# Stick-breaking attention: sums over later keys as two float32r products on the logits' bank, and a new order of the tail

## The chip, the cores and the metric

One core of one Trainium2 chip runs the whole program. The metric is the device time of one execution in microseconds (us).

## The reference, cut to what matters

Two small transformer blocks run one after the other on a sequence of 256 tokens of width 1024, all in float32. The last-but-one stage is stick-breaking attention with 16 heads of 64:

```python
def stick_breaking(h, w_in, q_gain, k_gain, w_o):
    q, k, v = jnp.split(h @ w_in, 3, axis=-1)
    q = rms_norm(heads(q), q_gain); k = rms_norm(heads(k), k_gain); v = heads(v)
    for blk in range(S // QB):                      # two blocks of 128 queries
        z = einsum('bhtd,bhsd->bhts', q[blk], k[:kend]) * scale
        mask = s_pos[None, :] < t_pos[:, None]
        log_stay = where(mask, log_sigmoid(-z), 0.0)
        later = cumsum(log_stay, axis=3, reverse=True) - log_stay
        weight = where(mask, exp(log_sigmoid(z) + later), 0.0)
        outs.append(einsum('bhts,bhsd->bhtd', weight, v[:kend]))
    return concatenate(outs) @ w_o
```

With softplus(z) = max(z, 0) + log(1 + exp(-|z|)), log_sigmoid(-z) is -softplus(z) and log_sigmoid(z) is z - softplus(z). So the weight of a key is exp(z - softplus(z) - sum of softplus over the later keys).

## The kernel before, in words

The tokens lie in two halves of 128 partitions. All weights stream from HBM in slabs of 128x2048 float32. Each slab is split into a float32r high part (cast on ACT, L168) and a low part (subtraction on VectorE, L169), and every product of the projections is made of three float32r matmuls (high-high, high-low, low-high: L271 to L273 for projections by columns, L294 to L300 for output products). A call of W.pump splits the next slab and sends off the load of another on SP's queue.

The framework (Tile) orders the instructions of TensorE, VectorE and POOL by itself, from the order in the program and its estimate of what is ready. It also hands out the buffers of a pool: those of one tag are given to the next tile in the order in which they come free. For stages 8 and 9 the ACT engine is taken out of that (L1388): ACT executes in the order in which the program is written.

Stage 8, `stick`, is the attention. Its projection `si` has six chunks of 512 columns, done in the order q (2), k 2, v 4, k 3, v 5. `both(c, ...)` (L1243) does one chunk in four steps (two slab halves times two token halves, twelve matmuls each), and after each step the attention work that is listed for it. Heads are taken in pairs, i = 0 to 7; e is the head in the pair. The logits z of one head are 128 keys by 3x128 columns: the second key block for the second query block, then the first key block for both query blocks. The work on a pair:

- `l1(i)` (L1158): mask and logits into the bank (L1168 to L1172, TensorE), then on ACT l = Abs(z), Exp(-l), Ln(1 + l) (L1186 to L1188). The banks are a two-bank tile, acc0 for even pairs and acc1 for odd ones; pair 6 takes the two `mm` banks of the projections.
- `l2(i)` (L1191), VectorE: sp = max(z, 0) + l, which is softplus (L1194), and l = min(z, 0) - l, which is log_sigmoid(z) (L1195).
- `w1(i)` (L1197): sums over later keys, float32 products of the constant `later` with sp, written over z in its bank (L1201 with 384 columns, L1202 with 128), then l = l - sum on VectorE (L1204).
- `w2(i)` (L1206), ACT: the weight, Exp(l) in place. The text calls it weight Exp(i).
- `pv(i)` (L1210): weights times v (L1222), then the split of the result into high and low parts for the output product (ACT L326, VectorE L327).

The tiles l and sp of pairs 0 to 5 come from the pool `k4` (one tag, four buffers of 4 KB per partition), which the other stages use too for their 4 KB tiles. Those of pairs 6 and 7 lie in one tile of the pool `xt`.

In the tail (L1280) `out(j, half)` is the j-th quarter of the output product for one token half, in acc0 or acc1, with pair work behind it. The next stage's first steps (residual, norm, transposes) follow.

Of the kernel before, what the change touches and what calls it, by code (L numbers as in the profile page):

```python
# [11 lines left out]
F32 = mybir.dt.float32  # L12
F32R = mybir.dt.float32r
# [5 lines left out]
P = 128  # L19
# [172 lines left out]
def tile_two_models(ctx: ExitStack, tc: tile.TileContext, a: dict):  # L192
# [3 lines left out]
    def pool(name, bufs, **kw):  # L196
        return ctx.enter_context(tc.tile_pool(name=name, bufs=bufs, **kw))
# [3 lines left out]
    part_pool = pool("part", SLOTS)  # L201
    xt_pool = pool("xt", 1)
    k8 = pool("k8", 1)
    k4 = pool("k4", 4)
    k2 = pool("k2", 4)
    wk = pool("wk", 2)
    sm = pool("sm", 4)
# [35 lines left out]
    def power(dst, src, add):  # L243

        n = src.shape[-1]
        t = small(n, tag=f"pw{n}")
        V.tensor_scalar(t, src, add, None, ALU.add)
        G.tensor_tensor(dst, t, nhalf[:, 0:n], ALU.pow)

    def junk(n):  # L250
        return wk.tile([P, D], mybir.dt.bfloat16, tag="junk", name="junk", bufs=1)[:, 0:n]
# [125 lines left out]
    def add_normed(gb, weight):  # L377
        def update(half, acc, factor=None):
            eps = EPS / weight**2 if factor is None else factor[1]
            ms = small(2, tag="ms2")  # L380
            y = k4.tile([P, D], F32, tag="k4", name="y")
# [46 lines left out]
    def ffn(tag, xT, rstd, skew=True, first=None, last_stage=False):  # L428
# [41 lines left out]
        def gated(c, b):  # L470

            if c not in hT:
                hT[c] = k4.tile([P, 2, 2, 2, P], F32R, tag="k4", name=f"hT{c}")
# [12 lines left out]
            V.tensor_tensor(hd, t[1], sg, ALU.mult)  # L486
            split_plain(hd, hT[c][:, :, 0, b], hT[c][:, :, 1, b])

        def tr(c, half):
            if c not in hT:  # L490
                hT[c] = k4.tile([P, 2, 2, 2, P], F32R, tag="k4", name=f"hT{c}")
# [114 lines left out]
    def conv(xT, rstd):  # L606
# [9 lines left out]
        def tr_u(c, half):  # L616
            if half not in uT:
                u = big((4, 0)[half], [P, 2048], F32, f"uT{half}")
                uT[half] = u[:, 0 : KD * (P + 2)].rearrange("p (k t) -> p k t", k=KD)
                cv[half] = k4.tile([P, KD, P], F32, tag="k4", name=f"cv{half}")  # L620
                if half == 0:
                    V.memset(uT[0][:, :, 0:2], 0.0)
            t = new_tr("tr_u")
# [99 lines left out]
    def attention(xT, rstd, xk, rstd_k, kT):  # L723
# [38 lines left out]
        def s1(g, half):  # L762
            nh, n = (4, P) if half == 0 else (2, 2 * P)
            ps = new_acc(g % 2, f"sc{half}{g}").rearrange("p (c h k) -> p h c k", h=nh, c=2)
            for i in range(nh):
                hd = g * nh + i
                for c in range(2):
# [4 lines left out]
            s = k4.tile([P, nh, 2, n], F32, tag="k4", name="s")  # L772
# [18 lines left out]
        def s3(g, half):  # L791
            nh, n, s, sums = st.pop((g, half))
            sv = sums.rearrange("p (h c) -> p h c", c=2)
            if half not in r0s:
                r0s[half] = small(8, tag=f"r0{half}")
                if half == 0:
                    asb[half] = k4.tile([P, 8, n], F32, tag="k4", name="aA")
# [143 lines left out]
    def retention(xT, rstd):  # L941
# [21 lines left out]
        rope = k4.tile([P, 2, 2, P], F32, tag="k4", name="rope")  # L963

        G.dma_start(rope, a["rope"].rearrange("p (a b t) -> p a b t", a=2, b=2))

# [59 lines left out]
            ys[hd, half] = y  # L1026

        def tr_y(hd, half):
            y = k4.tile([P, 2, 4, P], F32R, tag="k4", name=f"ryT{hd}_{half}")
# [71 lines left out]
    def stick(xT, rstd):  # L1101
# [17 lines left out]
        mask = k2.tile([P, 3 * P], F32, tag="k2", name="smask")  # L1119
        gq = small(tag="gq", bufs=1)  # L1120
        identr = wk.tile([P, 4 * P], F32R, tag="gb", name="sbr", bufs=1)
        later = wk.tile([P, 2 * P], F32, tag="sg", name="later")

        G.dma_start(mask, a["sb_mask"])
        G.dma_start(later, a["sb_later"])

        def setup():
            S.copy(identr[:, 0:P], ident)
            S.copy(identr[:, P : 4 * P], mask)
            V.scalar_tensor_tensor(gq, g_cols(G_SBQ, 1), 0.125, g_cols(G_SBK, 1), ALU.mult, ALU.mult)  # L1130

        def after(c, half, ps):
# [25 lines left out]
        def l1(i):  # L1158

            if i == 6:  # L1160
                zs = [new_mm() for _ in range(2)]
            else:
                z = new_acc(i % 2, f"z{i}")
                zs = [z[:, 0:512], z[:, 512:1024]]
# [6 lines left out]
            for e in range(2):  # L1171
                T.matmul(zs[e][:, P : 3 * P], k[pp[e], 0:P], q[pp[e], :], start=False, stop=True)  # L1172
            if i < 6:
                l, sp = (k4.tile([P, D], F32, tag="k4", name=n)[:, 0 : 6 * P] for n in ("l", "sp"))
            else:
                if i == 6:
                    st["last"] = xt_pool.tile([P, 2, 2, 6 * P], F32, tag="xT", name="l67")
                t = st["last"][:, i - 6]
                l, sp = t[:, 0], t[:, 1]
            l, sp = (t.rearrange("p (e t) -> p e t", e=2) for t in (l, sp))  # L1180
            if i == 6:
                zp = [(zs[e][:, 0 : 3 * P], l[:, e], sp[:, e]) for e in range(2)]
            else:
                zp = [(z.rearrange("p (e t) -> p e t", e=2)[:, :, 0 : 3 * P], l, sp)]
            for zz, ll, _ in zp:
# [3 lines left out]
            st[i] = zs, zp, l, sp  # L1189

        def l2(i):  # L1191

            for z, l, sp in st[i][1]:
                V.scalar_tensor_tensor(sp, z, 0.0, l, ALU.max, ALU.add)  # L1194
                V.scalar_tensor_tensor(l, z, 0.0, l, ALU.min, ALU.subtract)  # L1195

        def w1(i):  # L1197

            zs, zp, l, sp = st[i]
            for e in range(2):  # L1200
                T.matmul(zs[e][:, 0 : 3 * P], later[:, 0:P], sp[:, e], start=True, stop=False)  # L1201
                T.matmul(zs[e][:, 2 * P : 3 * P], later[:, P : 2 * P], sp[:, e, 0:P], start=False, stop=True)  # L1202
            for z, ll, _ in zp:
                V.tensor_tensor(ll, ll, z, ALU.subtract)  # L1204

        def w2(i):  # L1206
            l = st[i][2]
            S.activation(l, l, AF.Exp)

        def pv(i):  # L1210
            w = st.pop(i)[2]
            t = new_tr("tr_o")
            pp = [slice(0, 64), slice(64, P)]
            c = [slice((2 * i + e) * 64, (2 * i + e) * 64 + 64) for e in range(2)]
            steps = [
# [24 lines left out]
        def body():  # L1240
            nc.scalar.preload_act_table_set("natural_log_exp_and_others")

            def both(c, *todo):  # L1243
# [17 lines left out]
                [(pv, 2), (w2, 3), (l1, 5), (l2, 4)],  # L1261
                [(pv, 3), (w1, 4), (l2, 5)],
            )
            l1(6)

        def out(j, half, *todo):
            def run():
# [11 lines left out]

        tails = [  # L1280
            [
                out(0, 0, (w2, 4), (w1, 5), (l1, 7), (l2, 6)),
                out(1, 0, (w2, 5), (pv, 4), (w1, 6), (l2, 7)),
                lambda: (pv(5), w2(6), w1(7)),
                out(2, 0, (pv, 6), (w2, 7)),
                out(0, 1, (pv, 7)),
                out(3, 0),
            ],
# [5 lines left out]
    def start(make, gcols):  # L1294
        xT, rstd = {}, {}
        stage = make(xT, rstd)
        x_t = [k4.tile([P, 2, 4, P], F32, tag="k4", name=f"x_t{i}") for i in range(2)]
# [109 lines left out]
def constants():  # L1407
# [14 lines left out]
    seen = s_pos // 64 <= t_pos // 64  # L1422
    decay = np.exp(log_gamma[None, :, None] * np.abs(t_pos - s_pos)[:, None, :]) * seen[:, None, :]
    sb_mask = np.where(s_pos < t_pos, 0.0, -1e30).astype(f32)
    sb_later = np.concatenate([p[:, None] > p[None, :], np.ones((P, P))], axis=1).astype(f32)
    return {
        "neg_dist": neg_dist,
        "rope": rope,
# [22 lines left out]
```

## Time and profile before

| | us |
|---|---|
| median of 3 runs (1598.68 to 1600.39) | 1599.68 |
| the profiled execution | 1599.57 |
| its span, first to last instruction | 1597.6 |
| TensorE busy / VectorE / ACT in the span | 1564.9 / 1091.7 / 928.8 |
| stage 8 after its head, about | 1318 to 1412 |

The profiled execution took 2 us more than its span, for what lies before the first and after the last instruction. In the views, PE is TensorE's matmuls, PEld its weight loads, DVE VectorE, ACT ScalarE, SP the queue that issues the loads. A matmul's time in a row includes its drain, so matmuls overlap: the pace is the distance of the starts. A float32 product appears as two records. "x12" is several instructions of one line that follow each other; [1.70 <-PE z L1172] is idle time of the engine before the row and what ended it.

### The profile page before, as it was taken

Reading aid. Unit: us, or ns where it says so; the run is one execution under the profiler, and the core shown is the slowest. Engines: PE = TensorE matmul, PEld = TensorE weight load, DVE = VectorE, ACT = ScalarE, POOL = GpSimd, SP = SyncE. Lnnn points to the kernel's source line nnn. Section 1 sums busy time; section 2 is a strip of 40 time slices with the busy share of each in tenths; the row PEclk is TensorE's granted clock in tenths of the full one; section 3 lists DMA queues with packets and bytes.
Section 4 is the critical chain, followed back from the end, with each engine's and each line's share of the span. In section 5 each row is a group of like instructions: output and inputs, shape, how many; then the busy total and the mean of one; then the engine's idle time right before and its main releaser. Section 6 shows DMA issues by size and latency. Waiting matters only on the chain.

```text
span 1597.6 us, 21722 instructions
## 1 busy us (share of the span) xinstructions
PE 1564.9 (98%) x8408; PEld 1375.4 (86%) x8408; DVE 1091.7 (68%) x1757; ACT 928.8 (58%) x1623; POOL 61.1 (4%) x65
## 2 busy tenths in 40 slices
PE   6999999999999999989999999999999999999999
PEld 6899888899989999877899888888899988688997
DVE  7767767667687676788676776456667676666664
ACT  7655656555576555676555654456455576755552
POOL 0000100000000000101000010000000021000000
PEclk9999999999999999999999999999999999999999
DMA  8755644555655555444555555545455553235551
GB/s 308 254 193 209 235 151 181 198 211 192 207 179 201 211 200 206 159 167 147 183 198 205 212 203 184 185 147 196 160 209 195 207 213 133 105 132 211 207 192 49
DMA packets 42872, 300.94 MB, mean 188 GB/s; under 512 B 4800, under 2 KB 4928, under 8 KB 7312
## 3 DMA queue, kind: packets, MB, share of 16 engines
q1 hardware_dynamic: 42336, 297.91, 52.2%
q8 instruction: 66, 1.08, 0.3%
q0 software_dynamic: 432, 1.64, 0.3%
q14 instruction: 38, 0.31, 0.1%
HBM read 298.48 MB, written 1.05 MB: 187 GB/s over the span
## 4 chain that ended last, share of the span: by engine, by line
PE 88%; DVE 5%; ACT 4%; issue 1%; POOL 1%; DMA 0%; SPq 0%; ACTq 0%; POOLq 0%
PE mm L462 25%; PE mm L465 13%; PE acc L300 8%; PE acc L294 8%; PE acc L297 8%; PE mm L271 7%; PE mm L273 7%; PE mm L272 7%; DVE wlo L169 2%; PE tr L587 1%; ACT whi L168 1%; POOL r L389 1%; PE tr_x L335 1%; PE z L1201 1%; ACT s L786 1%
## 5 line engine op out<-in xcount | busy, mean ns | idle before, releaser
L169 DVE TENSOR_TENSOR wlo<-raw,whi 128x1024 fp32r<-128x1024 f32 x532 | 635.5, 1221 | 324.4 <-ACT whi L168 323.8
L168 ACT CAST whi<-raw 128x1024 fp32r<-128x1024 f32 x532 | 539.7, 1050 | 333.6 <-issue 134.3
L462 PE MATMUL mm<-xT,whi 128*128 128x512 f32 x1856 | 606.3, 383 | 12.5 <-DVE xT L320 12.5
L465 PE MATMUL mm<-xT,wlo 128*128 128x256 f32 x1856 | 469.6, 273 | 0.0
L462 PEld LDWEIGHTS mm<-xT,whi 128*128 128x128 f32 x1856 | 338.6, 190 | 51.2 <-DVE xT L320 12.4
L465 PEld LDWEIGHTS mm<-xT,wlo 128*128 128x128 f32 x1856 | 355.7, 192 | 12.4
L271 PE MATMUL mm<-whi,xT 128*128 128x512 f32 x456 | 178.9, 392 | 0.6 <-ACT xT L318 0.6
L273 PE MATMUL mm<-whi,xT 128*128 128x512 f32 x456 | 173.4, 380 | 0.0
L272 PE MATMUL mm<-wlo,xT 128*128 128x512 f32 x456 | 173.1, 380 | 0.0
L294 PE MATMUL acc<-whi,hT 128*128 128x512 f32 x516 | 153.8, 380 | 0.0
L300 PE MATMUL acc<-whi,hT 128*128 128x512 f32 x516 | 153.7, 379 | 0.0
L297 PE MATMUL acc<-wlo,hT 128*128 128x512 f32 x516 | 153.5, 379 | 0.0
L297 PEld LDWEIGHTS acc<-wlo,hT 128*128 128x128 f32 x516 | 97.5, 189 | 13.8
L300 PEld LDWEIGHTS acc<-whi,hT 128*128 128x128 f32 x516 | 97.5, 189 | 13.8
L294 PEld LDWEIGHTS acc<-whi,hT 128*128 128x128 f32 x516 | 97.4, 189 | 12.2
L271 PEld LDWEIGHTS mm<-whi,xT 128*128 128x128 f32 x456 | 86.2, 189 | 14.9 <-issue 2.3
L273 PEld LDWEIGHTS mm<-whi,xT 128*128 128x128 f32 x456 | 86.2, 189 | 13.4 <-DVE xT L320 1.0
L272 PEld LDWEIGHTS mm<-wlo,xT 128*128 128x128 f32 x456 | 86.3, 189 | 11.8 <-issue 1.0
L478 ACT COPY part<-mm 128x256 f32<-128x256 f32 x116 | 42.9, 370 | 56.3 <-PE mm L462 56.3
L326 ACT CAST hT<-hid 128x256 fp32r<-128x256 f32 x116 | 46.9, 404 | 28.0 <-DVE hid L486 27.9
L486 DVE TENSOR_TENSOR hid<-gated,sg 128x256 f32<-128x256 f32 x116 | 49.3, 425 | 12.1 <-DVE gated L484 0.5
L483 ACT COPY part<-mm 128x256 f32<-128x256 f32 x116 | 43.1, 371 | 19.7 <-PE mm L462 19.6
(243 smaller groups left out, 1614.5 us busy)
## 6 DMA issues: line engine op xcount, KB each, us to landing
raw<-in_w SPq DMA_DIRECT2D x277, 1024.0 KB, 4.8
gb<-in_norm_g SPq DMA_DIRECT2D x6, 512.0 KB, 5.6
raw<-in_w SPq DMA_DIRECT2D x2, 512.0 KB, 6.5
h<-in_x SPq DMA_DIRECT2D x2, 512.0 KB, 9.9
dec<-in_decay POOLq DMA_DIRECT2D x1, 768.0 KB, 6.6
x_t<-in_x_t SPq DMA_DIRECT2D x2, 256.0 KB, 4.5
x_t<-in_x_t SPq DMA_DIRECT2D x1, 512.0 KB, 7.7
out<-h SPq DMA_DIRECT2D x1, 512.0 KB, 2.6
```

Source lines behind the costliest of these rows:

```text
L168: self.nc.scalar.copy(hi[:, c], raw[:, c])
L169: self.nc.vector.tensor_tensor(lo[:, c], raw[:, c], hi[:, c].bitcast(F32), ALU.subtract)
L271: T.matmul(o, xh, wh, start=start, stop=False)
L272: T.matmul(o, xh, wl, start=False, stop=False)
L273: T.matmul(o, xl, wh, start=False, stop=stop)
L294: T.matmul(acc[:, n * 512 : n * 512 + 512], xh(kts + k), columns(wh, c), start=st, stop=False)
L297: T.matmul(acc[:, n * 512 : n * 512 + 512], xh(kts + k), columns(wl, c), start=False, stop=False)
L300: T.matmul(acc[:, n * 512 : n * 512 + 512], xl(kts + k), columns(wh, c), start=False, stop=sp[n])
L326: S.copy(hi, tr)
L462: T.matmul(ps[n], wh[:, w], x2, start=kk == 0, stop=kk == 7, skip_group_check=True)
L465: T.matmul(o, wl[:, w], x2[:, 0], start=False, stop=False, skip_group_check=True)
L486: V.tensor_tensor(hd, t[1], sg, ALU.mult)
```

## The change

The sums are no longer written over the logits but added to them. The constant is negated and includes the key itself (>= for >), so that the bank holds z - softplus(z) - sum over later keys after the products, and the weight is Exp of the bank. softplus is split into a high and a low part in float32r, with one product for each. For that:

- `l2` makes softplus in place in l (one pass), then the parts hi (ACT copy) and lo (VectorE subtraction) by `split_plain`; the pass that made log_sigmoid goes.
- `w1` has eight float32r products per pair in place of four float32 ones, and no subtraction behind them.
- `w2` reads the bank and writes l.
- The constant is loaded as float32 and copied to float32r by ACT in `setup`, in two buffers of the tag `sg`.
- The pool `k4` has two tags, a and b, of two buffers each. Other stages' tiles alternate between the two; l takes a, hi and lo take b. Pairs 6 and 7 keep l in `xt`, which is smaller now.
- Pair 7's logits lie in two banks of the transposes' pool. The results of pv(4) and pv(5) lie in acc1, those of pv(6) and pv(7) in `mm` banks.
- Weight Exp(4) comes before l1(6), and the tail has a new order.

```diff
-    k4 = pool("k4", 4)
+    k4_pool = pool("k4", 2)
...
+    n_k4 = [0]
+
+    def k4(shape, dtype, name, side=None):
+
+        if side is None:
+            side = "ab"[n_k4[0] % 2]
+            n_k4[0] += 1
+        return k4_pool.tile(shape, dtype, tag=f"k4{side}", name=name)
...
-        later = wk.tile([P, 2 * P], F32, tag="sg", name="later")
+        later_in = wk.tile([P, 2 * P], F32, tag="sg", name="later_in")
+        later = wk.tile([P, 2 * P], F32R, tag="sg", name="later")
...
-        G.dma_start(later, a["sb_later"])
+        G.dma_start(later_in, a["sb_later"])
...
+            S.copy(later, later_in)
...
+            elif i == 7:
+                zs = [new_tr("mm") for _ in range(2)]
...
-                l, sp = (k4.tile([P, D], F32, tag="k4", name=n)[:, 0 : 6 * P] for n in ("l", "sp"))
+                l = k4([P, 6 * P], F32, f"l{i}", "a")
...
-            for z, l, sp in st[i][1]:
-                V.scalar_tensor_tensor(sp, z, 0.0, l, ALU.max, ALU.add)
-                V.scalar_tensor_tensor(l, z, 0.0, l, ALU.min, ALU.subtract)
+            zs, zp, l = st[i]
+            for z, ll in zp:
+                V.scalar_tensor_tensor(ll, z, 0.0, ll, ALU.max, ALU.add)
+            hi, lo = (k4([P, 6 * P], F32R, f"{n}{i}", "b").rearrange("p (e t) -> p e t", e=2) for n in ("sph", "spl"))
+            split_plain(l, hi, lo)
+            st[i] = zs, zp, l, hi, lo
...
-            zs, zp, l, sp = st[i]
+            zs, zp, l, *parts = st[i]
             for e in range(2):
-                T.matmul(zs[e][:, 0 : 3 * P], later[:, 0:P], sp[:, e], start=True, stop=False)
-                T.matmul(zs[e][:, 2 * P : 3 * P], later[:, P : 2 * P], sp[:, e, 0:P], start=False, stop=True)
-            for z, ll, _ in zp:
-                V.tensor_tensor(ll, ll, z, ALU.subtract)
+                for sp in parts:
+                    T.matmul(zs[e][:, 0 : 3 * P], later[:, 0:P], sp[:, e], start=False, stop=False, skip_group_check=True)
+                for n, sp in enumerate(parts):
+                    T.matmul(
+                        zs[e][:, 2 * P : 3 * P], later[:, P : 2 * P], sp[:, e, 0:P], start=False, stop=n == 1,
+                        skip_group_check=True,
+                    )
+            st[i] = zs, zp, l
...
-            l = st[i][2]
-            S.activation(l, l, AF.Exp)
+            for z, ll in st[i][1]:
+                S.activation(ll, z, AF.Exp)
...
-            t = new_tr("tr_o")
+            if i in (4, 5):
+                if i == 4:
+                    st["banks"] = new_acc(1, "tr_o")
+                t = st["banks"][:, (i - 4) * 512 : (i - 3) * 512]
+            else:
+                t = new_mm() if i > 5 else new_tr("tr_o")
...
+            w2(4)
             l1(6)
...
-                out(0, 0, (w2, 4), (w1, 5), (l1, 7), (l2, 6)),
-                out(1, 0, (w2, 5), (pv, 4), (w1, 6), (l2, 7)),
-                lambda: (pv(5), w2(6), w1(7)),
-                out(2, 0, (pv, 6), (w2, 7)),
+                out(0, 0, (w1, 5), (l1, 7), (w2, 5), (l2, 6)),
+                out(1, 0, (pv, 4), (w1, 6), (w2, 6), (l2, 7)),
+                lambda: pv(5),
+                out(2, 0, (pv, 6), (w1, 7), (w2, 7)),
...
-    sb_later = np.concatenate([p[:, None] > p[None, :], np.ones((P, P))], axis=1).astype(f32)
+    sb_later = -np.concatenate([p[:, None] >= p[None, :], np.ones((P, P))], axis=1).astype(f32)
```

Left out here are the renamed calls: every `k4.tile([...], tag="k4", name=n)` of the other stages is now `k4([...], dtype, n)`.

## Rows read from the trace of the kernel before

**Rows 1.** The page, part 1: busy us of each engine, share of the span, instructions.

```profile
PE 1564.9 (98%) x8408; PEld 1375.4 (86%) x8408; DVE 1091.7 (68%) x1757; ACT 928.8 (58%) x1623; POOL 61.1 (4%) x65
```

**Rows 2.** Windows, one stretch: length; busy of PE, PEld, DVE, ACT, POOL; PEclk; DMA.

```profile
1369.00:1381.00 12.00, 12.00 (x81) 8.84 (x80) 6.88 (x9) 9.05 (x14) 0.00 (x0) 1.00 0.37 113
```

**Rows 3.** Timeline of ACT, 1361 to 1389: start, us, engine, line, operation [idle before].

```profile
1361.39 0.82 ACT L1186 ACTIVATE l<-z 128x768 f32<-128x768 f32 x1
...
1363.87 1.98 ACT L168 CAST whi<-raw 128x1024 fp32r<-128x1024 f32 x2
1369.21 1.07 ACT L1153 COPY skT<-tr 128x512 f32<-128x512 f32 x2 [3.36 <-PE tr L587]
...
1372.73 0.81 ACT L1186 ACTIVATE l<-z 128x768 f32<-128x768 f32 x1 [1.70 <-PE z L1172]
...
1378.85 0.27 ACT L326 CAST xk<-tr_o 128x128 fp32r<-128x128 f32 x1 [0.94 <-DVE xk L327]
...
1382.22 0.67 ACT L1134 ACTIVATE sv<-mm,rstd 128x512 f32<-128x512 f32 x1
...
1383.53 0.27 ACT L326 CAST xk<-tr_o 128x128 fp32r<-128x128 f32 x1 [0.49 <-DVE xk L327]
...
1385.59 0.87 ACT L1186 ACTIVATE l<-mm 128x384 f32<-128x384 f32 x2
...
1388.12 0.83 ACT L1208 ACTIVATE l<-l 128x768 f32<-128x768 f32 x1
```

**Rows 4.** Timeline of PE, 1363 to 1378.

```profile
1368.58 1.04 PE L587 MATMUL tr<-ident,ev 128*128 128x128 f32 x8
1369.47 0.91 PE L1201 MATMUL z<-sp,later 128*128 128x384 f32 x2
1370.22 0.38 PE L1202 MATMUL z<-sp,later 128*128 128x128 f32 x2
1370.44 0.81 PE L1201 MATMUL z<-sp,later 128*128 128x384 f32 x2
...
1371.23 0.60 PE L1168 MATMUL z<-sbr 128*128 128x384 f32 x2
...
1372.61 0.48 PE L271 MATMUL mm<-whi,xT 128*128 128x512 f32 x1
...
1375.40 0.88 PE L1222 MATMUL tr_o<-l,sv 128*64 128x128 f32 x12
1376.21 0.62 PE L1168 MATMUL z<-sbr 128*128 128x384 f32 x2
```

**Rows 5.** Timeline of PE, 1378 to 1401.

```profile
1386.71 0.89 PE L294 MATMUL acc<-whi,xk 128*128 128x512 f32 x2
...
1397.99 0.88 PE L1222 MATMUL tr_o<-l,sv 128*64 128x128 f32 x12 [1.27 <-ACT l L1208]
...
1400.55 0.68 PE L294 MATMUL acc<-whi,xk 128*128 128x512 f32 x2
```

**Rows 6.** Groups by line and shape, 1333 to 1412: busy us, mean ns; idle before.

```profile
L1208 ACT ACTIVATE l<-l 128x768 f32<-128x768 f32 x8 | 6.8, 844 | 4.3 <-DVE l L1204 4.3
...
L1204 DVE TENSOR_TENSOR l<-l,z 128x768 f32<-128x768 f32 x7 | 6.6, 949 | 2.2 <-PE z L1202 2.2
```

**Rows 7.** Windows of 2 us, 708 to 716.

```profile
708.00:710.00 2.00, 0.35 (x2) 0.00 (x0) 1.09 (x3) 0.00 (x0) 1.80 (x1) 1.00 0.28 33
710.00:712.00 2.00, 0.13 (x1) 0.16 (x2) 1.79 (x3) 0.84 (x3) 0.00 (x0) 1.00 0.70 270
712.00:714.00 2.00, 2.00 (x8) 1.73 (x8) 0.70 (x4) 1.81 (x7) 0.00 (x0) 0.50 0.53 221
714.00:716.00 2.00, 2.00 (x11) 1.77 (x9) 1.28 (x3) 0.69 (x1) 0.00 (x0) 0.64 0.00 0
```

**Rows 8.** Timeline of ACT, 1395 to 1398.

```profile
1395.22 1.97 ACT L168 CAST sp<-raw 128x1024 fp32r<-128x1024 f32 x2
```

**Rows 9.** Timeline of PE, 1421.6 to 1422.

```profile
1421.65 0.38 PE L271 MATMUL mm<-sp,xT 128*128 128x512 f32 x1
```

More of the change, by code (lines that the diff above doesn't have):

```diff
@@ L380, in update @@
             ms = small(2, tag="ms2")
-            y = k4.tile([P, D], F32, tag="k4", name="y")
+            y = k4([P, D], F32, "y")
             c = [slice(0, 512), slice(512, D)]
@@ L472, in gated @@
             if c not in hT:
-                hT[c] = k4.tile([P, 2, 2, 2, P], F32R, tag="k4", name=f"hT{c}")
+                hT[c] = k4([P, 2, 2, 2, P], F32R, f"hT{c}")
             g, u = (o.rearrange("p (i a r) -> p i r a", i=2, r=2) for o in gu_ps.pop((c, b)))
@@ L490, in tr @@
             if c not in hT:
-                hT[c] = k4.tile([P, 2, 2, 2, P], F32R, tag="k4", name=f"hT{c}")
+                hT[c] = k4([P, 2, 2, 2, P], F32R, f"hT{c}")
             t = new_tr("tr_h")
@@ L619, in tr_u @@
                 uT[half] = u[:, 0 : KD * (P + 2)].rearrange("p (k t) -> p k t", k=KD)
-                cv[half] = k4.tile([P, KD, P], F32, tag="k4", name=f"cv{half}")
+                cv[half] = k4([P, KD, P], F32, f"cv{half}")
                 if half == 0:
@@ L771, in s1 @@
                     )
-            s = k4.tile([P, nh, 2, n], F32, tag="k4", name="s")
+            s = k4([P, nh, 2, n], F32, "s")
             bias = nd[:, 2 * P - n :].rearrange("p (o k) -> p o k", o=1).broadcast_to([P, 2, n])
@@ L796, in s3 @@
                 if half == 0:
-                    asb[half] = k4.tile([P, 8, n], F32, tag="k4", name="aA")
+                    asb[half] = k4([P, 8, n], F32, "aA")
                 else:
@@ L962, in retention @@
         scs = wk.tile([P, 2, 3 * P], F32, tag="gb", name="scs", bufs=1)
-        rope = k4.tile([P, 2, 2, P], F32, tag="k4", name="rope")
+        rope = k4([P, 2, 2, P], F32, "rope")
         G.dma_start(rope, a["rope"].rearrange("p (a b t) -> p a b t", a=2, b=2))
@@ L1028, in tr_y @@
         def tr_y(hd, half):
-            y = k4.tile([P, 2, 4, P], F32R, tag="k4", name=f"ryT{hd}_{half}")
+            y = k4([P, 2, 4, P], F32R, f"ryT{hd}_{half}")
             yT[hd, half] = y
@@ L1173, in l1 @@
             if i < 6:
-                l, sp = (k4.tile([P, D], F32, tag="k4", name=n)[:, 0 : 6 * P] for n in ("l", "sp"))
+                l = k4([P, 6 * P], F32, f"l{i}", "a")
             else:
                 if i == 6:
[L1177 to L1182, printed above, removed]
-            else:
-                zp = [(z.rearrange("p (e t) -> p e t", e=2)[:, :, 0 : 3 * P], l, sp)]
-            for zz, ll, _ in zp:
+                    st["last"] = xt_pool.tile([P, 2, 6 * P], F32, tag="xT", name="l67")
+                l = st["last"][:, i - 6]
+            l = l.rearrange("p (e t) -> p e t", e=2)
+            if i >= 6:
+                zp = [(zs[e][:, 0 : 3 * P], l[:, e]) for e in range(2)]
+            else:
+                zp = [(z.rearrange("p (e t) -> p e t", e=2)[:, :, 0 : 3 * P], l)]
+            for zz, ll in zp:
                 S.activation(ll, zz, AF.Abs)
@@ L1188, in l1 @@
             S.activation(l, l, AF.Ln, bias=1.0)
-            st[i] = zs, zp, l, sp
+            st[i] = zs, zp, l
         def l2(i):
-            for z, l, sp in st[i][1]:
-                V.scalar_tensor_tensor(sp, z, 0.0, l, ALU.max, ALU.add)
-                V.scalar_tensor_tensor(l, z, 0.0, l, ALU.min, ALU.subtract)
+            zs, zp, l = st[i]
[4 more added lines that the diff above has]
+            st[i] = zs, zp, l, hi, lo
         def w1(i):
-            zs, zp, l, sp = st[i]
+            zs, zp, l, *parts = st[i]
             for e in range(2):
-                T.matmul(zs[e][:, 0 : 3 * P], later[:, 0:P], sp[:, e], start=True, stop=False)
-                T.matmul(zs[e][:, 2 * P : 3 * P], later[:, P : 2 * P], sp[:, e, 0:P], start=False, stop=True)
-            for z, ll, _ in zp:
-                V.tensor_tensor(ll, ll, z, ALU.subtract)
+                for sp in parts:
[5 more added lines that the diff above has]
+                    )
+            st[i] = zs, zp, l
         def w2(i):
-            l = st[i][2]
-            S.activation(l, l, AF.Exp)
+            for z, ll in st[i][1]:
+                S.activation(ll, z, AF.Exp)
         def pv(i):
             w = st.pop(i)[2]
-            t = new_tr("tr_o")
+            if i in (4, 5):
[4 more added lines that the diff above has]
+                t = new_mm() if i > 5 else new_tr("tr_o")
             pp = [slice(0, 64), slice(64, P)]
@@ L1296, in start @@
         stage = make(xT, rstd)
-        x_t = [k4.tile([P, 2, 4, P], F32, tag="k4", name=f"x_t{i}") for i in range(2)]
+        x_t = [k4([P, 2, 4, P], F32, f"x_t{i}") for i in range(2)]
         Q.dma_start(x_t[0][:, 0], a["x_t"][0][:, 0:4])
```

## The prediction

> **What bounds the kernel now.** The page first: TensorE is busy for 98% of the span [rows 1], so nearly all the time is matmul time, and a change can give back only matmuls or TensorE's waits. The change lies in one stage, the stick-breaking attention (about 1336 to 1412 us), so the stage decides. A window of it says the same: in 12 us TensorE is busy for 12.0, ACT for 9.05 [rows 2]. ACT's timeline is the view to read next, because in this stage ACT runs in the written order: an ACT instruction that waits holds up everything behind it. Over one round, from Abs(3) at 1361.39 to the end of the weight Exp(4) at 1388.95, ACT spends 27.56 us, of which it waits 3.36, 1.70, 0.94 and 0.49 [rows 3]. So 21.1 us is work, and 6.5 us is all the slack that ACT has while TensorE passes through the same heads. TensorE's longest wait in the stage is the 1.27 us at pv(5) [rows 5]; w1(3), the logits of pair 4 and pv(2) follow each other without one [rows 4].
>
> **TensorE's saving.** The four float32 products of w1(3), 1369.47 to 1371.23, take 1.76 us; eight pairs make 14.1 us. The new w1 has eight float32r products. Four are wide: twelve projection products of 128x512 float32r lie between 1372.61 and 1375.40, so 0.23 us each at most, and 384 columns take 0.17. Four are narrow, and no float32r product with 128 columns is in the trace. Its nearest rows are, from below, the transposes, which also pass once over a 128x128 load, eight between 1368.58 and 1369.47, 0.11 each; from above, the float32 product of that width, 0.22 (1370.22 to 1370.44) [rows 4]. I take 0.11, since a wide float32r product costs a quarter of a wide float32 one (0.75, 1369.47 to 1370.22). Then w1 costs 4 x 0.17 + 4 x 0.11 = 1.12 us, and the change saves 0.64 x 8 = 5.1 us of TensorE; with 0.22 it is 1.56, and 1.6 us.
>
> **VectorE** loses two passes per pair (L1195, and L1204 at 0.95 us) and gains one of the same shape (the low part): 7.6 us less, on an engine that was not the limit [rows 6].
>
> **ACT's added work.** Each pair gets a rounding copy of 128x768, SBUF to SBUF. The weight Exp has that shape and takes 0.84 us [rows 6]; two casts of 128x1024 take 1.98 [rows 3], and three quarters of one is 0.74. I take 0.84, so 6.7 us in all and 3.4 in the round above (pairs 2 to 5). The weight Exp will read PSUM as Abs does, 0.82 [rows 3]: nothing.
>
> **ACT's added waits.** Three constraints are new.
> First, the bank of pair i was free for pair i+2 after VectorE's subtraction; now the weight Exp is its last reader. In the written order Abs(4) follows weight Exp(2) on ACT directly, and Abs(5) follows weight Exp(3). So ACT must wait while TensorE makes the logits, 1.38 us (1371.23 to 1372.61).
> Second, l gets two buffers of its own. Before, l(4) could take any free one of four, and Abs(4) at 1372.73 indeed ran ahead of pv(2) at 1375.40 [rows 3, 4]. Now it waits until pv(2) has read l(2): 0.81 us more of TensorE (1375.40 to 1376.21), also after weight Exp(2). Together 2.2 us and hand-overs, once for Abs(4) and once for Abs(5). If a projection's twelve matmuls stand in front, it is up to 2.8 more each. I take 2.5 each.
> Third, the copy hi(i) stands between two VectorE passes, and both parts share two buffers, so hi(3) waits for w1(2). After hi(2) come the low part 0.95, w1 1.12 and a drain of 0.2 (a narrow product is busy for 0.38 us though the next begins after 0.22), 2.3 us, of which the two casts between cover 1.98. VectorE may take pair 3's max first, 0.95 more. So 0.3 to 1.3; I take 1.0. For hi(5) after hi(4): the same 2.3, half the logits of pair 6 (0.7), less the work between on ACT (0.67 for v, two splits of 0.27, their 0.49), 1.7: that gives 1.3, or 0.6 without the logits and 2.2 with VectorE in the way. I take 1.4.
> The old waits for splits, 0.94 and 0.49, stay. Sum: 1.0 + 2.5 + 0.94 + 2.5 + 0.49 + 1.4 = 8.8 us. The copies of pairs 0 and 1 (1.7 us) also push Abs(3) back, by 0 to 1.9; I take 1.0.
>
> **The sum.** l1(6), 2.53 us (1385.59 to 1388.12) [rows 3], now comes behind weight Exp(4). The work of the round is 21.1 - 2.5 + 3.4 = 22.0, so weight Exp(4) ends at 1361.4 + 1.0 + 22.0 + 8.8 = 1393.2. The first output product needs its bank, and it started at 1386.71 [rows 5]: 6.5 us later. TensorE's saving turns into waiting, as it has nothing else to do by then.
> In the tail the third output block started 13.84 us after the first (1400.55) [rows 5]. Now ACT has to do in between l1(6), l1(7), weight Exp(5), hi(6), two casts, pv(4)'s splits, weight Exp(6), hi(7) and pv(5)'s splits: 2.5 + 2.5 + 0.8 + 0.8 + 2.0 + 1.0 + 0.9 + 0.8 + 1.3 = 12.6, with about 1.2 of waits 13.8. So the reordering (pair 7's logits early, in other banks) just pays for the copies. pv(6), 0.8, can be done by then: 0.8 less. Together 5.7 us more.
>
> **The clock.** Elsewhere in this kernel TensorE stood still for 3.52 us (busy 0.35 of 708 to 710 and 0.13 of 710 to 712); then the granted clock was 0.50 in 712 to 714 and 0.64 in 714 to 716, 1.2 for 2.4 GHz [rows 7]. That cost 2 x 0.5 + 2 x 0.36 = 1.7 us of matmul time. From weight Exp(3) to weight Exp(4) ACT now needs 2.5 + 2.5 + 0.8 + 1.7 + 1.4 + 0.8 + 2.0 + 0.8 = 12.5 us, and TensorE has for it three sets of logits (1.4 each), pv(3), w1(4) and w1(5), 7.2 us. A gap like that one is likely: 1.7 more.
> The Trainium skill, "TensorE: Matmul & The Clock Gate", section "HAM oscillation — how this bites in real kernels", lets each long gap start the next burst at the low clock; by that rule a second gap makes it +9.1 in place of +7.4, and the 1.27 us at pv(5) did not test it.
> So +7.4: 1599.57 for the profiled execution (0.11 under the median of the runs) gives **1607** us.
>
> **At nothing:** the copy of the constant stands in the head, long before w1(0). The two sides of the pool alternate as the four buffers did, so other stages keep their order. Later casts delay SP's loads behind them: the slab cast at 1395.22 [rows 8] is first used at 1421.65 [rows 9], which covers 7 us. POOL's two loads remain two.
>
> **Rivals.**
> (1) TensorE stays the bound: projection matmuls fill every wait, and ACT's slack of 6.5 us takes up the copies (3.4) and the rest. That needs the new waits held to 3 us of the 8.8, which is where it decides. Then 5.1 us less, 1594.5 (1598 with the narrow product at 0.22). For it: rows 1. Against it: Abs(4) and Abs(5) cannot start before TensorE has answered weight Exp(2) and (3). Chance of under 1596.5: 0.15.
> (2) A wash, the saving against part of the waits: 1596.5 to 1603, chance 0.15.
> (3) The waits come at their upper ends: 2.8 more at Abs(4), 0.9 at Abs(3), the narrow product at 0.22 on four steps of the chain (1.8), a second fall of the clock (1.7). Two of these make about 1611, all 1614. Chance 0.2.
> (4) float32r runs no faster than float32 with these operands: w1 doubles, 14 us more matmul, 1620 or so. The projections' float32r products speak against it [rows 4]. Chance 0.02.
> The forecast itself, 1603 to 1610, has 0.48. So slower 0.70, same 0.15, faster 0.15, with 0.2% (3.2 us) as what can be told from no change. The range leaves out about a tenth on either side: 1596 to 1614.
>
> **What would show it.** Right: ACT waiting 2 us or more on TensorE before Abs(4) and Abs(5); waits of several us of TensorE between 1372 and 1396 that ACT ends; the first output product after 1390; w1 at about 1.1 us; a granted clock under 1 in the stage. Wrong: Abs(4) without a wait, or TensorE as busy as before with a short w1; then rival 1 holds.

## The result and the profile after

The changed kernel takes **1612.33 us** (1611.85 to 1612.93, 4 runs) against 1600.04 in the same session: 1.0074 times as long, 95% interval 1.0062 to 1.0086. Run again later (e8 below) it took 1611.89, ratio 1.0067 (1.0055 to 1.0079). The forecast was 1607, slower, 1596 to 1614: direction and range hold, the size was 7.4 us where 12.3 were measured.

The page of the kernel after, part 1, answers to [rows 1]:

```profile
PE 1571.1 (98%) x8408; PEld 1381.0 (86%) x8408; DVE 1085.1 (67%) x1748; ACT 935.7 (58%) x1635; POOL 60.2 (4%) x65
```

The span grew by 12.3 us, to 1609.9, and TensorE's busy time by 6.2, though w1 has become cheaper. So part of the loss is matmuls that run longer, part is waiting.

**Where it arises.** The transposes of the norms (tr_x) are in both kernels and serve as milestones. PE's timeline before:

```profile
1290.37 1.04 PE L335 MATMUL tr_x<-ident,h 128*128 128x128 f32 x8
1415.59 1.04 PE L335 MATMUL tr_x<-ident,h 128*128 128x128 f32 x8
```

and after:

```profile
1292.37 1.04 PE L344 MATMUL tr_x<-ident,h 128*128 128x128 f32 x8
1427.87 1.04 PE L344 MATMUL tr_x<-ident,h 128*128 128x128 f32 x8
```

The first lies ahead of the attention, the second behind it. 2.00 us had been lost by the first, 12.28 by the second, and the span is 12.3 longer: the attention made **10.3 us**, what lies ahead of it 2.0, what lies behind it nothing.

**ACT after**, timeline, 1370 to 1401; it answers to [rows 3]. L1198 is Abs, L1227 the weight Exp, L335 with `sph` the copy hi, L335 with `xk` a split behind pv:

```profile
1370.04 0.84 ACT L335 CAST sph<-l 128x768 fp32r<-128x768 f32 x1 [1.26 <-DVE wlo L169]
1371.72 1.07 ACT L1164 COPY skT<-tr 128x512 f32<-128x512 f32 x2 [0.84 <-PE tr L596]
1372.68 0.83 ACT L1227 ACTIVATE l<-z 128x768 f32<-128x768 f32 x1
1378.73 0.81 ACT L1198 ACTIVATE l<-z 128x768 f32<-128x768 f32 x1 [5.22 <-PE tr_o L1246]
...
1384.85 0.27 ACT L335 CAST xk<-tr_o 128x128 fp32r<-128x128 f32 x1 [0.94 <-DVE xk L336]
...
1390.06 0.81 ACT L1198 ACTIVATE l<-z 128x768 f32<-128x768 f32 x1 [4.23 <-PE tr_o L1246]
...
1398.13 0.83 ACT L335 CAST sph<-l 128x768 fp32r<-128x768 f32 x1 [3.15 <-PE z L1219]
...
1400.76 0.80 ACT L1227 ACTIVATE l<-z 128x768 f32<-128x768 f32 x1
```

Abs(4) waits 5.22 us and Abs(5) 4.23, and the releaser of both is `tr_o`, the products pv(2) and pv(3): the wait for l's buffer ends last, not the one for the logits. Before, Abs(4) waited 1.70 for its logits [rows 3].

**TensorE after**, timeline, 1352 to 1403:

```profile
1352.08 0.39 PE L1217 MATMUL z<-sph,later 128*128 128x384 f32 x1
1352.31 0.34 PE L1217 MATMUL z<-spl,later 128*128 128x384 f32 x1
1352.48 0.22 PE L1219 MATMUL z<-sph,later 128*128 128x128 f32 x1
1352.54 0.27 PE L1219 MATMUL z<-spl,later 128*128 128x128 f32 x1
...
1371.88 0.42 PE L1217 MATMUL z<-sph,later 128*128 128x384 f32 x1
...
1372.99 0.28 PE L1219 MATMUL z<-spl,later 128*128 128x128 f32 x1
...
1374.43 0.60 PE L1185 MATMUL z<-sqT,skT 64*128 64x256 f32 x4
1374.96 0.48 PE L280 MATMUL mm<-whi,xT 128*128 128x512 f32 x1
...
1377.75 0.88 PE L1246 MATMUL tr_o<-l,sv 128*64 128x128 f32 x12
...
1383.81 0.44 PE L1181 MATMUL mm<-sbr 128*128 128x384 f32 x1 [2.40 <-ACT sv L1145]
...
1388.41 1.55 PE L1246 MATMUL tr_o<-l,sv 128*64 128x128 f32 x12
...
1393.39 0.69 PE L1217 MATMUL z<-sph,later 128*128 128x384 f32 x1 [1.24 <-ACT sph L335]
...
1402.37 1.16 PE L303 MATMUL acc<-whi,xk 128*128 128x512 f32 x2
```

TensorE was through with the logits of pair 4 when it began the next products at 1374.96, so Abs(4) could have had them at about 1375. But pv(2) stands behind the twelve products of a projection step (1374.96 to 1377.75), and ACT gets l's buffer when pv(2) is through. From there the delay comes back: the evacuation of v (L1145, which frees a bank of the projections) is queued on ACT behind pair 4, so TensorE has no bank for the next logits and stands still for 2.40 us. The twelve products of a pv take 0.88 us at 1377.75 (pv(2)) and 1.55 at 1388.41 (pv(3)): the clock has fallen in between. Windows after, columns as in [rows 2]:

```profile
1369.00:1381.00 12.00, 11.70 (x73) 9.73 (x74) 3.02 (x3) 4.83 (x7) 0.00 (x0) 1.00 0.25 87
1381.00:1393.00 12.00, 8.41 (x34) 4.63 (x33) 4.14 (x6) 6.77 (x11) 0.00 (x0) 0.65 0.27 89
1393.00:1405.00 12.00, 11.61 (x32) 8.84 (x33) 6.18 (x9) 8.13 (x15) 0.00 (x0) 0.50 0.11 37
1405.00:1417.00 12.00, 12.00 (x86) 10.22 (x85) 6.96 (x13) 8.78 (x17) 0.00 (x0) 1.00 0.36 140
```

The granted clock is at 0.50, 1.2 for 2.4 GHz, from about 1385 to 1405. ACT does not work more in this stretch: 6.77 us of 12, then 8.13. It waits for TensorE, and TensorE for ACT.

Groups after, 1333 to 1432, answer to [rows 6]:

```profile
L336 DVE TENSOR_TENSOR spl<-l,sph 128x768 fp32r<-128x768 f32 x8 | 7.6, 954 | 4.7 <-ACT sph L335 4.7
L335 ACT CAST sph<-l 128x768 fp32r<-128x768 f32 x8 | 6.6, 826 | 4.8 <-PE z L1219 3.1 <-DVE wlo L169 1.7
```

The eight copies cost ACT 6.6 us (6.7 forecast); VectorE's busy time fell by 6.6 (7.6 forecast).

### The profile page after: what moved, and what is told of

The parts are those of the page before. It is cut to its first block, busy times and chain, and to the rows that moved or that the text cites. A ratio compares the mean times of both kernels' runs of the same rounds, so it can differ in the third digit from the quotient of the medians.

```text
span 1609.9 us, 21737 instructions
## 1 busy us (share of the span) xinstructions
PE 1571.1 (98%) x8408; PEld 1381.0 (86%) x8408; DVE 1085.1 (67%) x1748; ACT 935.7 (58%) x1635; POOL 60.2 (4%) x65
## 4 chain that ended last, share of the span: by engine, by line
PE 85%; DVE 6%; ACT 4%; DMA 1%; issue 1%; POOL 1%; SPq 0%; ACTq 0%; POOLq 0%; DVEq 0%
PE mm L471 25%; PE mm L474 12%; PE acc L309 8%; PE acc L303 8%; PE acc L306 8%; PE mm L282 7%; PE mm L280 7%; PE mm L281 7%; DVE wlo L169 2%; DMA raw<-in_w 1%; ACT whi L168 1%; PE tr L596 1%; POOL r L398 1%; PE tr_x L344 1%; ACT s L795 1%
## 5 line engine op out<-in xcount | busy, mean ns | idle before, releaser
L474 PEld LDWEIGHTS mm<-xT,wlo 128*128 128x128 f32 x1856 | 355.7, 192 | 12.3
L309 PEld LDWEIGHTS acc<-whi,hT 128*128 128x128 f32 x516 | 97.5, 189 | 13.8
L335 ACT CAST hT<-hid 128x256 fp32r<-128x256 f32 x116 | 47.0, 405 | 28.0 <-DVE hid L495 27.9
## 6 DMA issues: line engine op xcount, KB each, us to landing
h<-in_x SPq DMA_DIRECT2D x2, 512.0 KB, 10.3
```

The source lines that it names most:

```text
L309: T.matmul(acc[:, n * 512 : n * 512 + 512], xl(kts + k), columns(wh, c), start=False, stop=sp[n])
L335: S.copy(hi, tr)
L474: T.matmul(o, wl[:, w], x2[:, 0], start=False, stop=False, skip_group_check=True)
```

## The experiments

Three theories went in. **A**: l's two buffers hold up ACT, and the gaps that follow take the clock down. **B**: ACT's eight copies are the cost. **C**: the low clock itself is most of the loss. Every kernel was timed against the kernel before on the same chip; a ratio has its 95% interval behind it.

### e1: a buffer more for l

```diff
-                l = k4([P, 6 * P], F32, f"l{i}", "a")
+                if i == 4:
+                    l = [k2.tile([P, 512], F32, tag="k2", name="l4")[:, 0 : 3 * P] for _ in range(2)]
+                else:
+                    l = k4([P, 6 * P], F32, f"l{i}", "a")
...
```

What is left out here does pair 4's Abs, Exp, Ln and splits by head, since its l now lies in two tiles.

> The changed kernel, with l of pair 4 in two free 2 KB buffers of another pool (one per head, so its Abs, Exp, Ln and splits go by head), so that Abs(4) no longer waits for pv(2), nor Abs(5) for pv(3). Theory A (l's two buffers hold up ACT because pv comes behind a projection step, and the gaps that follow take TensorE's clock down): ACT's wait before Abs(4) falls from 5.2 to about 1.7 us, the one before Abs(5) from 4.2 to about 1.7, TensorE's gap of 2.4 us at 1381 closes, and the time falls by 4 to 9 us, to 1603 to 1608. Theory B (ACT's eight added copies, 6.5 us, are the cost; the buffers are not): less than 2 us, 1610 to 1612. Theory C (the low clock is the cost, whatever starts it): the time follows the stretch at half clock, 20 us now; if that stays, so does the time.

Measured: **1603.40 us**, ratio 1.0018 (1.0009 to 1.0026); of the change's 1.0067 to 1.0074 some 8 to 9 us are gone, as theory A said. ACT's timeline of e1 (L1203 is Abs, in two halves for pair 4) and its windows:

```profile
1375.97 0.87 ACT L1203 ACTIVATE l<-z 128x384 f32<-128x384 f32 x2 [1.57 <-PE z L1185]
...
1384.78 0.81 ACT L1203 ACTIVATE l<-z 128x768 f32<-128x768 f32 x1 [1.76 <-PE z L1185]
```

```profile
1365.00:1369.00 4.00, 2.14 (x9) 1.69 (x10) 3.32 (x4) 3.01 (x4) 0.65 (x1) 0.95 0.00 0
1369.00:1373.00 4.00, 4.00 (x18) 3.44 (x18) 2.33 (x3) 1.23 (x2) 0.00 (x0) 0.62 0.33 104
1385.00:1389.00 4.00, 2.42 (x17) 1.39 (x14) 1.63 (x3) 3.83 (x7) 0.00 (x0) 1.00 0.26 104
1389.00:1393.00 4.00, 4.00 (x14) 3.19 (x13) 2.06 (x5) 2.44 (x4) 0.00 (x0) 0.51 0.00 0
```

Both waits are 1.6 to 1.8 us now and end with the logits. What is left are gaps of TensorE elsewhere (about 1.9 us in the first window, 1.6 in the third), and each was followed by a stretch at low clock in this profile, which is that of the slowest of the twelve executions. The twelve executions run from 1600.0 to 1606.2 us: the three with a mean clock of 0.998 took 1600.0 to 1600.5, the four with 0.995 took 1605.2 to 1606.2. (Two at 0.999 took 1602.4 and 1603.4, so the clock is not all of the spread.)

### e2: the gaps filled

```diff
+        def fill(n):
+            for _ in range(n):
+                T.matmul(st[4][0][0][:, 3 * P : 4 * P], ident, ident, start=False, stop=False, skip_group_check=True)
...
-                [(pv, 3), (w1, 4), (l2, 5)],
+                [(fill, 16), (pv, 3), (fill, 10), (w1, 4), (l2, 5)],
```

> The changed kernel, with 16 float32 products of 128x128 (3.5 us, into columns of pair 4's banks that nothing reads) behind the last projection step, where TensorE stands still for 2.4 us, and 10 more (2.2 us) behind pv(3). Theory C (the low clock is the cost): the granted clock stays at 1.00 from 1383 to 1405, pv(3) and the logits of pairs 5 and 6 take half as long, the first output product starts 4 to 6 us earlier and the time falls by 4 to 9 us, to 1603 to 1608. Theory A (the waits themselves are the cost): ACT's chain stays, with 2 us less of waiting before Abs(5) since the logits and pv(3) come faster; 0 to 3 us less. Theory B (ACT's load): no change, or up to 2 us more where the added products stand in the way.

Measured: **1606.77 us**, ratio 1.0045 (1.0032 to 1.0058). Windows of e2, then its ACT timeline:

```profile
1381.00:1393.00 12.00, 12.00 (x91) 9.60 (x90) 4.39 (x8) 6.08 (x12) 0.00 (x0) 1.00 0.25 89
1393.00:1405.00 12.00, 11.44 (x62) 8.64 (x60) 7.15 (x9) 11.58 (x17) 0.00 (x0) 1.00 0.25 89
```

```profile
1376.70 0.81 ACT L1198 ACTIVATE l<-z 128x768 f32<-128x768 f32 x1 [5.23 <-PE tr_o L1250]
...
1386.26 0.81 ACT L1198 ACTIVATE l<-z 128x768 f32<-128x768 f32 x1 [2.46 <-PE tr_o L1250]
...
1393.29 0.83 ACT L335 CAST sph<-l 128x768 fp32r<-128x768 f32 x1 [2.11 <-PE z L1219]
...
1395.92 0.80 ACT L1227 ACTIVATE l<-z 128x768 f32<-128x768 f32 x1
```

TensorE does 26 useless products more, and the kernel is faster. The clock stays at 1.00, the wait before Abs(4) is the same to the hundredth (5.23), those behind it shrink from 4.23 to 2.46 and from 3.15 to 2.11. By the milestones the attention loses 6.65 us in this profile, against 10.3 with the low clock (the program ahead of it stands at -0.04, the milestone behind it at +6.61). So with the clock held up 3.6 us come back by the profiles and 3.5 to 4.6 by the ratios. The time itself lies in the range that theory C gave, but most of the loss stays at full clock, so C is not the most of it. The clock's own share may be somewhat larger than 3.6: the ten added products behind pv(3) run from 1386.09 to 1388.34, ahead of logits of pairs 6 and 7, and the second product of w1(4) starts at 1392.12 behind such logits, although lo(4) was ready at about 1390.7. That is up to 1.4 us which the filling itself may cost; no run separates it. C explains a third of the 10.3 us, at most about half.

### e3: float32 in place of the split

```diff
-            hi, lo = (k4([P, 6 * P], F32R, f"{n}{i}", "b").rearrange("p (e t) -> p e t", e=2) for n in ("sph", "spl"))
-            split_plain(l, hi, lo)
...
+                T.matmul(zs[e][:, 0 : 3 * P], later[:, 0:P], l[:, e], start=False, stop=False, skip_group_check=True)
+                T.matmul(
+                    zs[e][:, 2 * P : 3 * P], later[:, P : 2 * P], l[:, e, 0:P], start=False, stop=True,
+                    skip_group_check=True,
+                )
```

> The changed kernel without the split: w1 takes softplus from l as one float32 operand, four float32 products per pair that accumulate on the logits, the constant stays float32; bank, buffers of l, order and tail as in the changed kernel. It gives back 0.62 us of TensorE per pair (5.0 in all) and takes away eight copies of ACT (6.5 us), eight subtractions of VectorE (7.6) and the waits before the copies (3.1 and 1.3). Theory A: Abs(4) and Abs(5) still wait 4 us or more, TensorE still has a gap of over 2 us and the clock falls; 1606 to 1612. Theory B (ACT's load): ACT keeps up, no gap of over 1.5 us, and the time goes back to 1599 to 1603. Theory C: 1600 to 1604 if the clock stays, 1608 or more if it falls.

The constant stays float32 too. Measured: **1605.26 us**, ratio 1.0031 (1.0019 to 1.0043): less than theory A said, more than B did. ACT's timeline of e3 (L1196 is Abs, L1238 pv):

```profile
1375.03 0.81 ACT L1196 ACTIVATE l<-z 128x768 f32<-128x768 f32 x1 [5.26 <-PE tr_o L1238]
```

Without any copy Abs(4) still waits 5.26 us for pv(2), TensorE still has a gap of 2.07, and the clock is low for some 10 us from 1388. So the buffers alone make the gap, but the copies cost too.

### e4: the two tags alone

The kernel before with this edit, and `l` in tag a, `sp` in tag b:

```diff
-    k4 = pool("k4", 4)
+    k4_pool = pool("k4", 2)
...
+    def k4(shape, dtype, name, side=None):
...
+        return k4_pool.tile(shape, dtype, tag=f"k4{side}", name=name)
```

> The kernel before, with its pool of four 4 KB buffers in two tags of two, as the changed kernel has it, l in the one and sp in the other; nothing else of the change. Of the 12.3 us that the changed kernel lost, 2.0 lay before the attention, most of it at about 910 to 925 us where ACT's casts waited for weight loads. If the two tags make that: the same 2.0 us more, 1602, with the shift at the same place. If it is how the loads fall in one program or another, or comes from the attention's other tiles: within 0.5 us of before. In the attention l has two buffers as in the changed kernel, but the bank is still released by VectorE: with theory A some of the waits of Abs(4) and Abs(5) show here too, 1 to 4 us more.

Measured: **1603.94 us**, ratio 1.0023 (1.0014 to 1.0031), 3.7 us more. ACT's timeline of e4 (L1195 is Abs, L1217 the weight Exp):

```profile
1368.70 0.86 ACT L1217 ACTIVATE l<-l 128x768 f32<-128x768 f32 x1
1375.58 0.81 ACT L1195 ACTIVATE l<-z 128x768 f32<-128x768 f32 x1 [6.02 <-PE tr_o L1231]
```

In a kernel that sums in float32, subtracts on VectorE and has no copies, two buffers for l are enough to make Abs(4) wait 6.02 us for pv(2). The shift ahead of the attention is -0.6 us in this profile, so the two tags alone need not bring the 2.0.

### e5: the copy on VectorE

```diff
-            split_plain(l, hi, lo)
+            V.tensor_copy(hi, l)
+            V.tensor_tensor(lo, l, hi.bitcast(F32), ALU.subtract)
```

> The changed kernel with the copy hi on VectorE in place of ACT (eight of 128x768); all else as in the changed kernel, l's two buffers too. ACT loses 6.5 us of work, VectorE gains some 7, and the way from max through hi and lo to w1 stays on one engine. Theory A (l's two buffers and the clock): Abs(4) still waits 4 us or more for pv(2), there is still a gap of over 2 us of TensorE and a stretch at half clock, and no more than 4 us comes back: 1608 to 1612. Theory B (ACT's added work): 5 to 9 us come back, 1603 to 1607, and the wait before Abs(4) only grows by what ACT is early.

Measured: **1605.95 us** (1603.15 to 1608.65), ratio 1.0031 (1.0019 to 1.0042). Some 6 us come back, as theory B said and A did not. ACT's timeline of e5 (L1247 is pv):

```profile
1376.59 0.81 ACT L1198 ACTIVATE l<-z 128x768 f32<-128x768 f32 x1 [8.18 <-PE tr_o L1247]
```

The wait before Abs(4) grew to 8.18 us, since ACT comes early to the same pv(2). TensorE's gap of 2.40 us and a stretch at half clock behind it (about 1384 to 1400) are still there, as A said. A is right about the buffers and was wrong in putting the copies below 4 us. How much comes back goes with the clock: the four executions with a mean clock of 0.997 took 1603.2 to 1604.8, the four with 0.992 to 0.995 took 1607.1 to 1608.7; the profile is one of the latter. The edit takes ACT's work away and also the hand-over between two engines; which of the two counts is not shown.

### e6 and e7: the buffer, and no copy on ACT

e6 has the edits of e1 and e5, e7 those of e1 and e3.

> Both: l of pair 4 in two buffers of its own, and the copy hi on VectorE. Theory A: with the buffer the copies are the next term, as ACT's chain from Abs(3) to weight Exp(4) is then 3.4 us shorter; TensorE's gaps at 1365 (1.3 and 0.7 us) and 1387 shrink and with them the stretches at half clock: 1597 to 1601, 2 to 5 us less than with the buffer alone. If the low clock comes from gaps that stay: 1602 to 1604, as with the buffer alone.

> The changed kernel without the split (four float32 products of l per pair, accumulated on the logits) and with pair 4's l in two buffers of its own. It has neither the two-buffer limit nor the copies; what is left of the change is that the bank is released by the weight Exp and the new order of the tail, less VectorE's work. Theory A: the time goes back to that of before or a little over, 1598 to 1602. If the later release of the bank alone costs much: 1603 to 1606.

Measured: e6 **1598.26 us**, ratio 0.9995 (0.9983 to 1.0007), one of twelve executions at 1607.8 with a mean clock of 0.994; e7 **1598.64 us**, ratio 0.9989 (0.9981 to 0.9998). Together the two terms are the whole loss, some 12 us; alone they gave back 8 to 9 (e1) and some 6 (e5), so they overlap. e7 keeps the bank's later release and the new tail and is no slower than before, so these two parts of the change, with the passes that VectorE no longer makes, cost nothing that shows. e6 has 4 to 5 us less of matmuls than e7 and is not faster: in its profile TensorE still waits 1.55 us for lo(3) (at 1368 to 1370) behind two splits of a weight slab on VectorE; the clock stays at 1.00 behind this gap.

### e8: the change again

> The changed kernel itself once more, for more runs and a second profile: 1611 to 1613. If the 2.0 us before the attention lie in how the weight loads fall from execution to execution, the shift at 925 us comes out otherwise in this profile and the runs spread by 1 to 3 us; if they belong to the program, 2.0 us again at the same place. Theory C (the low clock is the cost): the stretch at half clock is again some 20 us long from about 1385.

Measured: 1611.89 us (1610.83 to 1612.27). Ahead of the attention this profile stands at +1.69, and it got there much as the first one did: by 467 us the two stand at 0.93 and 0.81, from 925 on at 1.69 and 2.00. That is nearer to what was expected if it belongs to the program. The experiments on the changed kernel, which are the same up to the attention (but for the constant in e3 and e7), stood between -0.7 and +2.9 there, one profile each, and what is late are weight loads (in the first profile ACT's casts wait 2.13 us at 909.78 and 3.03 at 921.75 for them). That speaks for the way the loads fall and against a part of the change, but it is not shown; the 2.0 us stay open. The attention loses 10.7 us this time, with the clock at 0.50 from 1385 to 1405.

### e9: a version that beats both

e6, with one split of a weight slab moved:

```diff
-                    if n % 2:
+                    if n % 2 and (c, n) != (3, 3):
                         W.pump(1)
...
-                [(tr, 3, 0), (tr, 3, 1), (w2, 2), (w1, 3), (l1, 4)],
+                [(tr, 3, 0), (tr, 3, 1), (w2, 2), (w1, 3), (W.pump, 1), (l1, 4)],
```

> The kernel with pair 4's l in two buffers of its own and hi on VectorE, and one more edit: the split of the weight slab that stood between max(3), hi(3) and lo(3) on VectorE (two casts of 1.2 us) is asked for after w1(3), where ACT waits for the logits of pair 4 anyway. The 1.55 us that TensorE waits for lo(3) at 1368 go, and with them what started the clock's fall in some executions. Theory A: 1595 to 1597.5, the runs closer together. If the later cast makes the load behind it late: up to 2 us more than without the edit, 1598 to 1600.

Measured: **1597.85 us** (1597.00 to 1601.12), ratio **0.9983** (0.9974 to 0.9992): 2.8 us under the kernel before in the same session, 14 under the change. Windows of e9:

```profile
1369.00:1381.00 12.00, 11.74 (x72) 8.78 (x71) 7.56 (x13) 9.39 (x17) 0.00 (x0) 1.00 0.39 126
1381.00:1393.00 12.00, 11.57 (x66) 9.02 (x65) 7.27 (x11) 11.09 (x19) 0.00 (x0) 1.00 0.35 138
1393.00:1405.00 12.00, 11.87 (x88) 9.34 (x88) 6.42 (x13) 5.71 (x13) 0.00 (x0) 1.00 0.25 89
```

The weight casts now fill ACT's wait before Abs(4), TensorE's longest wait in the stage is 0.43 us, and the clock stays up in this profile. The time is 0.35 us above the range that theory A gave. The ratio is under 1 by more than its interval; against e6 the intervals overlap, so what the moved split gives by itself is not shown.

### e10: pv ahead of the projection

```diff
-                [(tr, 3, 0), (tr, 3, 1), (w2, 2), (w1, 3), (l1, 4)],
-                [(pv, 2), (w2, 3), (l1, 5), (l2, 4)],
-                [(pv, 3), (w1, 4), (l2, 5)],
+                [(tr, 3, 0), (tr, 3, 1), (w2, 2), (w1, 3), (pv, 2), (l1, 4)],
+                [(w2, 3), (pv, 3), (l1, 5), (l2, 4)],
+                [(w1, 4), (l2, 5)],
```

> The changed kernel with pv(2) and pv(3) listed ahead of the logits that follow them, so that pv(2) does not stand behind the twelve products of a projection step; l keeps its two buffers. Theory A: the wait before Abs(4) falls from 5.2 to 2.2 to 2.7 us (pv 0.8, logits 1.4, hand-overs), the one before Abs(5) from 4.2 to 2.2 to 2.7; TensorE's gap at 1381 falls under 2 us; 3 to 7 us less, 1605 to 1609, more where the clock stays up. If the projection in front is not what made the waits long: 1610 to 1613.

Measured: **1604.40 us**, ratio 1.0021 (1.0012 to 1.0030), just under theory A's 1605 to 1609. ACT's timeline of e10:

```profile
1375.39 0.27 ACT L335 CAST xk<-tr_o 128x128 fp32r<-128x128 f32 x1 [0.98 <-PE tr_o L1246]
1376.02 0.27 ACT L335 CAST xk<-tr_o 128x128 fp32r<-128x128 f32 x1 [0.36 <-DVE xk L336]
1376.85 0.81 ACT L1198 ACTIVATE l<-z 128x768 f32<-128x768 f32 x1 [0.57 <-PE z L1185]
```

With the same two buffers, and pv(2) and pv(3) only listed earlier, ACT waits 1.9 us in three pieces before Abs(4) in place of 5.2, and the last of them ends with the logits. The projection step in front of pv(2) was what made the wait long. A later gap (1.61 us before w1(4)) still takes the clock down for about 10 us.

## Why the prediction was right in direction and short in size

**Right.** The mechanism: ACT in written order, held up before Abs(4) and Abs(5) by l's two buffers and the bank, TensorE's saving turned into waiting. One head's four products of w1 take 0.57 us where they follow another head's (1352.08 to 1352.65, the last counted at 0.11), so 1.14 for a pair; w1(3), whose eight stand together, takes 1.22 (1371.88 to 1373.10). 1.12 was forecast, and that it came so near is partly luck: the wide products take 0.23 and 0.17, not 0.17 each, the narrow ones 0.06 and 0.11, not 0.11 each, and the two errors nearly cancel. VectorE's and ACT's added and removed work were right to 1 us.

**Waits of the round**, Abs(3) to weight Exp(4), in us:

| wait | forecast | after | e2, clock at 1.00 |
|---|---|---|---|
| hi(3) | 1.0 | 1.26 | 1.26 |
| copies of kT | 0 | 0.84 | 0.84 |
| Abs(4) | 2.5 | 5.22 | 5.23 |
| splits | 0.94, 0.49 | 0.94, 0.63 | 0.94, 0.63 |
| Abs(5) | 2.5 | 4.23 | 2.46 |
| hi(5) | 1.4 | 3.15 | 2.11 |
| sum | 8.8 | 16.3 | 13.5 |

Abs(3) came 0.2 us later than before (1363.60 less 2.0, against 1361.39 in [rows 3]), not the 1.0 of the forecast.

**The step that failed first** is "Together 2.2 us and hand-overs ... I take 2.5 each". For Abs(5) it was exact where the clock held (2.46); there, too, a step is listed ahead of pv(3), but TensorE had done it while ACT waited before Abs(4). For Abs(4) the case named beside it came true, "If a projection's twelve matmuls stand in front, it is up to 2.8 more": 5.23 is 2.5 and 2.73. The order of the program had that step listed ahead of pv(2), and [rows 4] show its twelve products there (1372.61 to 1375.40), so this end should have been the value for Abs(4), and 2.5 the lower bound.

**The second** is the clock, "A gap like that one is likely: 1.7 more". The gap came (2.40 us), but the stretch at half clock was 20 us long, not the two windows of [rows 7], and cost about 3.6, or somewhat more (e2): some 9 us of matmul time (TensorE was busy for some 18 of the 20), of which the rest must have fallen into waits that were there anyway. The Trainium skill, "TensorE: Matmul & The Clock Gate", section "HAM oscillation — how this bites in real kernels", lets each long gap start the next burst at the low clock. In this trace the gap of 2.40 us was followed by a granted clock of 0.50, but the later gap (1.24 us at 1392) fell inside a stretch that had not ended, so it could not show a second fall. The price worked out beside it, +9.1, is nearer to the 10.3 than mine, by luck.

**The tail** was mis-sized in two terms that nearly cancel. The first output product came 13.7 us later (1402.37, less 2.0, against 1386.71 in [rows 5]), not 6.5; but w1(5) and the logits of pair 7 were put in front of it, and the third block started 8.63 us after the first (1411.00), not 13.8. What lies behind the third block takes 1.8 us longer. 13.7 - 5.2 + 1.8 = 10.3; at full clock in e2 10.1 - 5.3 + 1.9 = 6.7, against 5.7 forecast without the clock. So waits and tail together were 1 us off, the clock 2, and the 2.0 ahead of the attention were not in the forecast at all. That the first two came out so close is luck: the waits alone were 4.7 too small (13.5 in e2 against 8.8), and the tail's new order took most of that back.

**Rivals.** Rival 3, 1611 to 1614, is what happened, by the two of its terms that it names first and last (Abs(4), the clock). The total reaches its range only with the 2.0 us ahead of the attention, which it did not name; the attention's 10.3 alone make 1609.9, the upper edge of the forecast's own 1603 to 1610. Rival 1 fell: it needed the 8.8 us of waits held to 3, and they came to 16.3. Rival 4 fell with w1 at 1.1 to 1.2. Of what was put "at nothing", the later casts cost nothing that shows (behind the attention the shift stays at 12.3); for the other stages' order it is open, with the 2.0 us.

**The float32r products** themselves neither hurt nor help in the changed kernel. With the waits gone, the version with them (e9, 0.9983) and the one without (e7, 0.9989) have intervals that overlap; of 4 to 5 us of matmuls some 2 show in the profiles (the attention gains 3.8 us in e9 and 1.5 in e7), and e9 has the moved split besides.

## What to carry to other kernels

When a change takes buffers from a tile, look in the trace for the instruction that frees it and count what stands ahead of that instruction in its own engine's queue: this is the price, and it is there even if the data are ready. Price a gap of the engine that bounds the kernel as the gap and, where TensorE is that engine, a possible stretch at half clock behind it, and don't take the stretch's length from one instance. Here every gap of 2.07 to 2.40 us in the attention was followed by one (the change twice, e3, e5); of two gaps of about 1.55 us the one in e5 was, the one in e6 was not. Before giving up a cheaper computation, give the one tile that waits another buffer: here two idle 2 KB buffers and moving the copy to the engine that idles took back the 12 us (e6), and with one split moved besides there was a small gain (e9).

## What was not expected of the hardware

- A 128x128 float32r product behind one with the same weights starts 0.06 us after it (1352.48 to 1352.54), the next one 0.11 later; the bounds I had were 0.11 to 0.22.
- VectorE makes the float32r copy of 128x768 in 0.55 us (554 ns mean in e9), ACT in 0.83 (826 ns after). In the attention of the changed kernel VectorE was the idler one, too.
- TensorE's gaps of 1.31 and 0.69 us at 1365 to 1369 were followed by a low clock in e1's profile (0.62 over 1369 to 1373) and by none in the changed kernel's, where the same two gaps stand (1366.94 and 1368.93, clock 1.00). Stretches at half clock lasted from under 4 us (the first in e1) to 20 (the change), and the executions of one program differ in them: e6 took 1597.7 us at a mean clock of 0.999 and 1607.8 at 0.994.
